# Changes of stage in a hybrid encoder trunk: the second token tile's transposes queued behind the next stage's matmuls with the first

## The chip, the cores and the metric

The kernel runs on one NeuronCore of a Trainium2 chip, with TensorE (matmuls and transposes), VectorE, ScalarE, GpSimd and the DMA queues of that core. The metric is the device time of one execution in microseconds (us); the time before is the median of three runs.

## What is computed

The reference is an encoder of four layers over 256 tokens of 1024 features, in float32. Layer i has a token mixer (0 and 3: a bidirectional Mamba-2 SSD; 1: a bidirectional gated DeltaNet, "gdn"; 2: a bidirectional S5 with a GLU output) and a SwiGLU network ("ffn"). Each is wrapped in two RMS norms:

```python
def rms_norm(x, w):
    y = xf * lax.rsqrt(jnp.mean(xf * xf, axis=-1, keepdims=True) + NORM_EPS)
    return y * w
def reference(x, norm_w, ...):
    h = x
    for i in range(DEPTH):                      # 4
        hn = rms_norm(h, norm_w[i, 0])
        m = mixer(i % 3)(hn)                    # ssd, gdn, s5, ssd
        h = h + rms_norm(m, norm_w[i, 1])
        f = swiglu_ffn(rms_norm(h, norm_w[i, 2]), w_gate_up[i], w_down[i])
        h = h + rms_norm(f, norm_w[i, 3])
    return h
```

## The kernel before

**Data.** The residual `h` stays in SBUF with tokens on partitions, as two token tiles (t = 0 and 1) of 128 tokens. A stage's input is the normed `h`, transposed: features on partitions, 8 chunks k of 128, tokens along the row (256). Products are kept near float32: every operand is split into a high part and the rest, both in float32r, and a product is three matmuls (high by high, high by low, low by high). For activations the parts are `xh` (ScalarE, L191) and `xl` (VectorE, L192), for weights `whi` (ScalarE, L79) and `wlo` (VectorE, L80), from `raw`, which SyncE's queue loads (`weights`, L66 to L82).

**Stages.** ssd0, ffn0, gdn1, ffn1, s5 2, ffn2, ssd3, ffn3, written one after the other. Beside ffn0 and ffn1 run pieces of `s5_prep`, tables for the s5 stage (`s5c`, `tab`, `p`), woven in. A stage ends in `leave` (L226) for each token tile: `rms` (L209: two squares with a sum on ScalarE into a scratch tile, `ms` on VectorE, `rs`, the power -1/2, on GpSimd), then for each half of 512 features `mt` = result times `rs` times norm weight (L236) and `h` = `h` + `mt` (L237). It goes on into the next stage at once. For ffn, `enter_half` (L262) makes `xn` = `h` times norm weight (L266) with the token's scale left for later (`rq`, from `enter_scale`, L269). For the other stages, `enter` (L279) takes a second `rms` first and scales `xn` (L287). `turned` (L249) then transposes `xn`, four blocks into one tile `ht` (L255), and splits it into `xh` and `xl`; for s5 it copies to `s5x`.

**First matmuls of a stage.** In `ffn`, block f takes 8 chunks with 512 weight columns (gate and up of 256 features); tokens are the stationary operand, so one matmul covers one token tile with 512 columns. In block 0 the order is tile 0 for all k (24 matmuls) and then tile 1 (24). In `ssd` and `gdn` `project` (L133) makes the weights the stationary operand and streams all 256 tokens, 128 output features at a time: first the 128 features of dt (`ssd_wdt`, L449) or of a and b (`gdn_wab`, L572), 24 matmuls, then two times 24 for the 256 of `pb` (L466) or `pqk` (L610) of the first group. `dtx` (L451, L574), which the softplus chain on VectorE begins with, reads the first of these.

**Order.** Each engine works through its own queue in a fixed order. The order is set at build time by a scheduler that simulates the program, not by the lines of the source alone; tiles of a pool with few buffers add waits until the buffer's last reader is done.

Of the kernel before, what the change touches and what calls it, by code (L numbers as in the profile page):

```python
# [42 lines left out]
class Trunk:  # L43
    def __init__(self, ctx, tc, t):
        self.tc, self.nc, self.t = tc, tc.nc, t
        nc = self.nc
        pool = lambda name, bufs, **kw: ctx.enter_context(tc.tile_pool(name=name, bufs=bufs, **kw))
        self.cp = pool("const", 1)
        self.wk = pool("wk", 2)
        self.dr = pool("dr", 1, space=bass.MemoryType.DRAM)  # L50
        cp = self.cp
        self.ident = cp.tile([P, P], F32, name="ident")
        nc.gpsimd.dma_start(self.ident, t["c_ident"])
        self.ones = cp.tile([P, 1], F32, name="ones")
# [29 lines left out]
    def mmt(self, out, w, x, first, last, **kw):  # L84

        nc = self.nc
        nc.tensor.matmul(out, x[0], w[0], start=first, stop=False, **kw)  # L87
        nc.tensor.matmul(out, x[1], w[0], start=False, stop=False, **kw)  # L88
        nc.tensor.matmul(out, x[0], w[1], start=False, stop=last, **kw)  # L89

    def mm3(self, out, w, m, x, first, last, **kw):
        nc = self.nc
        hi, lo = (v[:, m * P:(m + 1) * P] for v in w)
        nc.tensor.matmul(out, hi, x[0], start=first, stop=False, **kw)  # L94
        nc.tensor.matmul(out, hi, x[1], start=False, stop=False, **kw)  # L95
        nc.tensor.matmul(out, lo, x[0], start=False, stop=last, **kw)  # L96

# [111 lines left out]
    def rms(self, parts, scale=1.0 / 32):  # L209

        nc = self.nc
        ss = self.wk.tile([P, 2], F32, name="ss", tag="ss", bufs=4)
        for j, p in enumerate(parts):
            sq = self.wide("sq")
            nc.scalar.activation(sq, p, AF.Square, scale=scale, accum_out=ss[:, j:j + 1])
        ms, r = (self.wk.tile([P, 1], F32, name=n, tag=n + "1", bufs=4) for n in ("ms", "rs"))
        nc.vector.scalar_tensor_tensor(out=ms, in0=ss[:, 0:1], scalar=EPS, in1=ss[:, 1:2], op0=ALU.add, op1=ALU.add)  # L217
        nc.gpsimd.tensor_tensor(out=r, in0=ms, in1=self.mhalf[:, 0:1], op=ALU.pow)  # L218
        return r

    def leave_to(self, nxt):


        nc = self.nc

        def leave(t, w, parts, scale=1.0 / 32, q=None):  # L226
            r = self.rms(parts, scale)
            if q is not None:
                r2 = self.wk.tile([P, 1], F32, name="r2", tag="r2", bufs=2)
                nc.vector.tensor_tensor(out=r2, in0=r, in1=q, op=ALU.mult)  # L230
                r = r2
            nw = self.norm_weight(w)
            for j, p in enumerate(parts):
                o = slice(512 * j, 512 * j + 512)
                m = self.wide("mt")
                nc.vector.scalar_tensor_tensor(out=m, in0=p, scalar=r[:, 0:1], in1=nw[:, o], op0=ALU.mult, op1=ALU.mult)  # L236
                nc.vector.tensor_tensor(out=self.h[:, t, o], in0=self.h[:, t, o], in1=m, op=ALU.add)  # L237
                if nxt is None:
                    (nc.sync, nc.scalar)[j].dma_start(self.out[t * P:t * P + P, o], self.h[:, t, o])
                elif nxt[0] == "ffn":  # L240
                    self.enter_half(t, j, nxt[1])
            if nxt is not None and nxt[0] == "ffn":
                self.enter_scale(t)
            elif nxt is not None and nxt[0] != "s5":
                self.enter(t, nxt[1])

        return leave

    def turned(self, t, j, xn, keep=None):  # L249
# [9 lines left out]
        else:  # L259
            self.split(self.xh[:, o[0], o[1]], self.xl[:, o[0], o[1]], pt)  # L260

    def enter_half(self, t, j, w):  # L262

        o = slice(512 * j, 512 * j + 512)
        xn = self.wide("xn")
        self.nc.vector.tensor_tensor(out=xn, in0=self.h[:, t, o], in1=self.norm_weight(w)[:, o], op=ALU.mult)  # L266
        self.turned(t, j, xn)

# [10 lines left out]
    def enter(self, t, w, keep=None):  # L279

        nc = self.nc
        nw = self.norm_weight(w)
        r = self.rms([self.h[:, t, 0:512], self.h[:, t, 512:]])
        for j in range(2):
            o = slice(512 * j, 512 * j + 512)
            xn = self.wide("xn")
            nc.vector.scalar_tensor_tensor(out=xn, in0=self.h[:, t, o], scalar=r[:, 0:1], in1=nw[:, o], op0=ALU.mult,  # L287
                                           op1=ALU.mult)
            self.turned(t, j, xn, keep)


    def ffn(self, i):
        nc, t_ = self.nc, self.t
# [3 lines left out]
        def block(f):  # L297

            w = self.weights(t_["w_gu"][i, f])
            ps = [self.pp.tile([P, 512], F32, name="proj", tag="proj") for _ in range(2)]  # L300
            order = [(t, k) for t in range(2) for k in range(KD)] if f < 1 else [(t, k) for k in range(KD) for t in range(2)]
            for t, k in order:
                self.mmt(ps[t], w[k], (tok(self.xh, k, t), tok(self.xl, k, t)), k == 0, k == KD - 1)
            return ps
# [20 lines left out]
        for f in range(FFB):  # L325
            ps = block(f)
# [106 lines left out]
    def ssd(self, i):  # L433
# [14 lines left out]

        ps = self.project(t["ssd_wdt"][j])  # L449
        x = wk.tile([P, L], F32, name="dtx", tag="t1", bufs=3)  # L450
# [13 lines left out]
        def into(g):  # L464

            pb = self.project(t["ssd_w"][j, g, 2])  # L466
            yield
# [86 lines left out]
    def gdn(self, i):  # L554
# [16 lines left out]

        ps = self.project(t["gdn_wab"])  # L572
        x = wk.tile([P, L], F32, name="dtx", tag="t1", bufs=3)
# [7 lines left out]
        for k in range(2):  # L581
            nc.tensor.transpose(pt[:, k], gb[:, k * P:(k + 1) * P], self.ident)
        gbt = wk.tile([P, 2, P], F32, name="dttok", tag="dttok", bufs=1)
        nc.vector.tensor_copy(gbt, pt)
# [24 lines left out]
        def into(a):  # L609
            pq = self.project(t["gdn_w"][a, 0], name="pqk")  # L610
            yield
# [48 lines left out]
        def base(a):  # L660
# [114 lines left out]
        def apply(a):  # L775
# [159 lines left out]
    def s5_prep(self, pr, first, last):  # L935
# [133 lines left out]
    def s5(self, i):  # L1069
# [179 lines left out]
def trunk(tc, ins, out, steps):  # L1249
    with ExitStack() as ctx:  # L1250
# [8 lines left out]

        k.out, k.rq, k.nwp = out, {}, ctx.enter_context(tc.tile_pool(name="nwp", bufs=2))  # L1260
        pre = lambda kind, i: 4 * i + (2 if kind == "ffn" else 0)
        post = lambda kind, i: pre(kind, i) + 1
        for n, (kind, i) in enumerate(steps):
            np_, nm = BANKS[kind][:2]
            with ExitStack() as c2:
# [106 lines left out]
```

## Time and profile before

| | us |
|---|---|
| median of 3 runs | 2035.88 |
| the runs | 2028.07, 2036.38, 2035.88 |
| the profiled execution | 2029.43 |
| its span, first to last instruction | 2027.7 |
| TensorE busy | 1782.4 |
| VectorE busy | 1441.8 |
| ScalarE busy | 1044.9 |
| GpSimd busy | 353.7 |
| mean granted TensorE clock | 0.932 of full |

The profile is of one execution; all rows shown are from it. A row of a timeline begins with its start in us from the span's start and its duration; consecutive instructions of one kind are one row with a count (x4). Square brackets give how long the engine stood idle before the row and which instruction let it go. A matmul's duration overlaps the next one's, so what one costs in a series is the distance between two starts. PE is TensorE, PEld its weight loads, DVE VectorE, ACT ScalarE, POOL GpSimd, SP SyncE.

### The profile page before, as it was taken

What the parts mean: (1) busy time and instruction counts of PE and PEld (TensorE: products, weight loads), DVE (VectorE), ACT (ScalarE), POOL (GpSimd) and SP (SyncE); (2) the same over time, 40 slices, a digit from 0 to 9 for tenths busy, and PEclk for the clock granted to TensorE, in tenths of its full rate; (3) what the DMA queues carried; (4) which work ended last, traced back from release to release, by engine and by line L of the source; (5) the groups of instructions that cost most, each with busy time, mean ns of one, the idle gap of its engine ahead of it and who ended that gap; (6) DMA issues with size and microseconds to landing.
All of it is one profiled execution on the core that took longest, in us unless ns stands there. A gap on an engine that the chain in (4) does not pass through costs nothing.

```text
span 2027.7 us, 35637 instructions
## 1 busy us (share of the span) xinstructions
PE 1782.4 (88%) x13948; PEld 1526.6 (75%) x13948; DVE 1441.8 (71%) x2542; ACT 1044.9 (52%) x1888; POOL 353.7 (17%) x536
## 2 busy tenths in 40 slices
PE   5999969999599988975999976969997999978998
PEld 5899848888588877763878765658886899857886
DVE  5999957997788676434989458456646999946653
ACT  4777746553466556423545334444434677734442
POOL 1121110000167465621000002010001111110000
PEclk9999979999799999986999966979998999988999
DMA  6344335776344343612767587256644334416652
GB/s 230 118 134 146 115 105 163 243 223 210 120 138 133 99 122 101 182 46 102 236 201 238 175 302 194 68 198 186 187 152 163 125 130 141 127 52 202 185 185 93
DMA packets 105848, 317.66 MB, mean 157 GB/s; under 512 B 11036, under 2 KB 35180, under 8 KB 103632
## 3 DMA queue, kind: packets, MB, share of 16 engines
q1 hardware_dynamic: 99472, 296.03, 45.6%
q0 software_dynamic: 5920, 18.83, 3.1%
q8 instruction: 109, 1.79, 0.4%
q14 instruction: 59, 0.48, 0.1%
q10 hardware_dynamic: 288, 0.52, 0.1%
HBM read 287.49 MB, written 27.85 MB: 156 GB/s over the span
## 4 chain that ended last, share of the span: by engine, by line
PE 71%; DVE 11%; POOL 5%; ACT 5%; issue 4%; DMA 3%; SPq 0%; DVEq 0%; POOLq 0%; ACTq 0%
PE proj L87 10%; PE proj L88 10%; PE proj L89 10%; PE acc_o L87 5%; PE acc_o L88 5%; PE acc_o L89 5%; PE proj L94 5%; PE proj L95 4%; PE proj L96 4%; DVE wlo L80 3%; PE yp L525 2%; POOL ybt L696 2%; ACT whi L79 2%; POOL yb L698 1%; DMA s_w<-wt 1%
## 5 line engine op out<-in xcount | busy, mean ns | idle before, releaser
L80 DVE TENSOR_TENSOR wlo<-raw,whi 128x1024 fp32r<-128x1024 f32 x475 | 599.3, 1267 | 242.2 <-ACT whi L79 235.3
L79 ACT CAST whi<-raw 128x1024 fp32r<-128x1024 f32 x475 | 495.0, 1049 | 413.5 <-PE proj L88 180.8
L87 PE MATMUL proj<-whi,xh 128*128 128x512 f32 x768 | 307.7, 403 | 23.9 <-DVE xl L192 20.0
L89 PE MATMUL proj<-wlo,xh 128*128 128x512 f32 x768 | 304.2, 396 | 0.0
L88 PE MATMUL proj<-whi,xl 128*128 128x512 f32 x768 | 304.2, 396 | 0.0
L94 PE MATMUL proj<-xh,whi 128*128 128x256 f32 x792 | 232.7, 295 | 9.2 <-DVE acc L421 5.0
L96 PE MATMUL proj<-xh,wlo 128*128 128x256 f32 x792 | 229.4, 290 | 0.0
L95 PE MATMUL proj<-xl,whi 128*128 128x256 f32 x792 | 227.3, 287 | 0.0
L87 PEld LDWEIGHTS proj<-whi,xh 128*128 128x128 f32 x768 | 147.2, 192 | 57.5 <-DVE xl L192 21.6
L87 PE MATMUL acc_o<-whi,yh 128*128 128x512 f32 x448 | 179.6, 404 | 5.8 <-ACT yh L191 5.8
L218 POOL TENSOR_TENSOR rs<-ms,mhalf 128x1 f32<-128x1 f32 x32 | 20.9, 653 | 935.0 <-DVE ms L217 930.8
L88 PE MATMUL acc_o<-whi,yl 128*128 128x512 f32 x448 | 179.2, 400 | 0.0
L89 PE MATMUL acc_o<-wlo,yh 128*128 128x512 f32 x448 | 176.3, 396 | 0.0
L89 PEld LDWEIGHTS proj<-wlo,xh 128*128 128x128 f32 x768 | 146.8, 191 | 31.4 <-issue 0.2
L88 PEld LDWEIGHTS proj<-whi,xl 128*128 128x128 f32 x768 | 147.2, 192 | 30.9 <-issue 0.7
L94 PEld LDWEIGHTS proj<-xh,whi 128*128 128x128 f32 x792 | 155.0, 196 | 15.6 <-DVE acc L421 5.8
L95 PEld LDWEIGHTS proj<-xl,whi 128*128 128x128 f32 x792 | 155.3, 196 | 0.1
L96 PEld LDWEIGHTS proj<-xh,wlo 128*128 128x128 f32 x792 | 155.0, 196 | 0.3
L408 ACT ACTIVATE e<-bc,csn 128x256 f32<-128x256 f32 (+1 forms) x320 | 108.7, 430 | 39.0 <-PE bc L403 39.0
L255 PE MATMUL ht<-ident,xn 128*128 128x128 f32 x128 | 29.2, 381 | 108.8 <-DVE xn L287 48.1
L421 DVE SCALAR_TENSOR_TENSOR acc<-proj,cw,acc 128x255 f32<-128x255 f32 (+1 forms) x256 | 118.3, 476 | 2.0
L500 POOL TENSOR_TENSOR e<-e,cbm 128x768 f32<-128x768 f32 x32 | 60.7, 1897 | 324.1 <-DVE cbm L852 130.7
(357 smaller groups left out, 3416.8 us busy)
## 6 DMA issues: line engine op xcount, KB each, us to landing
raw<-w_gu SPq DMA_DIRECT2D x176, 512.0 KB, 4.5
raw<-ssd_w SPq DMA_DIRECT2D x96, 512.0 KB, 3.8
raw<-w_dn SPq DMA_DIRECT2D x88, 512.0 KB, 3.6
raw<-gdn_w SPq DMA_DIRECT2D x48, 512.0 KB, 4.2
raw<-ssd_wo SPq DMA_DIRECT2D x32, 512.0 KB, 3.5
nwb<-norm_w POOLq DMA_DIRECT2D x16, 512.0 KB, 5.1
s_w<-wt SPq DMA_DIRECT2D x16, 512.0 KB, 5.4
s_cl<-clb SPq DMA_DIRECT2D x16, 512.0 KB, 5.2
```

Of the source, the lines that this page charges most:

```text
L79: nc.scalar.copy(hi, raw)
L80: nc.vector.tensor_tensor(out=lo, in0=raw, in1=hi.bitcast(F32), op=ALU.subtract)
L87: nc.tensor.matmul(out, x[0], w[0], start=first, stop=False, **kw)
L88: nc.tensor.matmul(out, x[1], w[0], start=False, stop=False, **kw)
L89: nc.tensor.matmul(out, x[0], w[1], start=False, stop=last, **kw)
L94: nc.tensor.matmul(out, hi, x[0], start=first, stop=False, **kw)
L95: nc.tensor.matmul(out, hi, x[1], start=False, stop=False, **kw)
L96: nc.tensor.matmul(out, lo, x[0], start=False, stop=last, **kw)
L408: nc.scalar.activation(e[:, o], src, AF.Relu, scale=-1.0, bias=n)
L421: nc.vector.scalar_tensor_tensor(out=acc[:, a:b], in0=ps[:, m, a + o:b + o], scalar=cw[:, k:k + 1], in1=acc[:, a:b], op0=ALU.mult, op1=ALU ...
L500: (nc.gpsimd if hl % 2 == 0 else nc.vector).tensor_tensor(out=es[hl], in0=es[hl], in1=cbm, op=ALU.mult)
L525: nc.tensor.matmul(yp[64 * hh:64 * hh + 64, m, a:b], xdt[:, s, d, 2 * m + hh], es[2 * m + hh][:, o:o + b - a], start=(n == 0), stop=(n == 3))
```

## The change

`turn` puts tile 1's transposes on a list; `turn_late` writes them behind the last matmul of the next stage that works on tile 0, with `issue_after`, which orders them on TensorE. In `ffn` that is between the two halves of block 0. For `ssd` and `gdn` the new `project_first` makes the first two projections token tile by token tile: 72 matmuls of 128 columns for tile 0, the transposes, 72 for tile 1. For s5 the transposes stay where they were. `leave` multiplies by the norm weight before `rs` is there, and takes the scale and the addition in one operation. The squares go to one fixed tile, `xn` gets a pool of two buffers, and to make room several tiles share or lose buffers. The weight casts are given no place in the order; the scheduler sets it.

```diff
+        self.junk = cp.tile([P, 512], F32, name="junk")
...
+    def project_first(self, srcs, names):
+
+        ws = [self.weights(v) for v in srcs]
+        out = [self.pp.tile([P, 2, L], F32, name=n, tag="proj") for n in names]
+        for t in range(2):
+            o = slice(t * P, t * P + P)
+            if t:
+                self.turn_late(mm)
+            for w, ps, src in zip(ws, out, srcs):
+                for m in range(src.shape[2] // P):
+                    for k in range(KD):
+                        mm = self.mm3(ps[:, m, o], w[k], m, (self.xh[:, k, o], self.xl[:, k, o]), k == 0, k == KD - 1)
+        return out
...
-            sq = self.wide("sq")
-            nc.scalar.activation(sq, p, AF.Square, scale=scale, accum_out=ss[:, j:j + 1])
+            nc.scalar.activation(self.junk, p, AF.Square, scale=scale, accum_out=ss[:, j:j + 1])
...
             r = self.rms(parts, scale)
+            nw = self.norm_weight(w)
+            ms = [self.wide("mt") for _ in parts]
+            for j, p in enumerate(parts):
+                nc.vector.tensor_tensor(out=ms[j], in0=p, in1=nw[:, 512 * j:512 * j + 512], op=ALU.mult)
...
-            nw = self.norm_weight(w)
-            for j, p in enumerate(parts):
+            for j, m in enumerate(ms):
                 o = slice(512 * j, 512 * j + 512)
-                m = self.wide("mt")
-                nc.vector.scalar_tensor_tensor(out=m, in0=p, scalar=r[:, 0:1], in1=nw[:, o], op0=ALU.mult, op1=ALU.mult)
-                nc.vector.tensor_tensor(out=self.h[:, t, o], in0=self.h[:, t, o], in1=m, op=ALU.add)
+                nc.vector.scalar_tensor_tensor(out=self.h[:, t, o], in0=m, scalar=r[:, 0:1], in1=self.h[:, t, o],
+                                               op0=ALU.mult, op1=ALU.add)
...
+    def turn(self, t, j, xn):
+
+        if t:
+            self.late.append((t, j, xn))
+        else:
+            self.turned(t, j, xn)
+
+    def turn_late(self, last):
+
+        with self.tc.issue_after(last.ins):
+            for v in self.late:
+                self.turned(*v)
+        self.late = []
+
     def enter_half(self, t, j, w):
...
-        xn = self.wide("xn")
+        xn = self.xnp.tile([P, 512], F32, name="xn", tag="xn")
...
-        self.turned(t, j, xn)
+        self.turn(t, j, xn)
...
             for t, k in order:
-                self.mmt(ps[t], w[k], (tok(self.xh, k, t), tok(self.xl, k, t)), k == 0, k == KD - 1)
+                if f < 1 and (t, k) == (1, 0):
+                    self.turn_late(mm)
+                mm = self.mmt(ps[t], w[k], (tok(self.xh, k, t), tok(self.xl, k, t)), k == 0, k == KD - 1)
...
-        ps = self.project(t["ssd_wdt"][j])
+        ps, pb0 = self.project_first([t["ssd_wdt"][j], t["ssd_w"][j, 0, 2]], ("proj", "proj"))
...
-            pb = self.project(t["ssd_w"][j, g, 2])
+            pb = self.project(t["ssd_w"][j, g, 2]) if g else pb0
...
-        ps = self.project(t["gdn_wab"])
+        ps, pq0 = self.project_first([t["gdn_wab"], t["gdn_w"][0, 0]], ("proj", "pqk"))
...
-            pq = self.project(t["gdn_w"][a, 0], name="pqk")
+            pq = self.project(t["gdn_w"][a, 0], name="pqk") if a else pq0
...
-                off = wk.tile([P, 2, P], F32, name="off", tag="off", bufs=7)
+                off = wk.tile([P, 2, P], F32, name="off", tag="off", bufs=6)
...
-            toep = pr.tile([P, P], F32, name="toep", tag="toep", bufs=2)
+            toep = pr.tile([P, P], F32, name="toep", tag="toep", bufs=1)
...
+        k.xnp, k.late = ctx.enter_context(tc.tile_pool(name="xnp", bufs=2)), []
...
-                k.slot = {"gdn": ("u", 3), "s5": ("u1", 2)}.get(kind, ("n5", 4))
+                k.slot = {"gdn": ("u", 3), "s5": ("u1", 2)}.get(kind, ("n5", 2))
```

Left out here: `enter` takes `turn` in the same way unless it keeps `s5x`; `mmt` and `mm3` return their last matmul; `dttok` of gdn shares the buffers of `lx`, `ysq` those of `yo`, and `s5bg` a wide slot. Lines of the changed kernel stand some 15 to 35 further down: `ht` L271, `xh` and `xl` L206 and L207, `whi` and `wlo` L80 and L81, `mt` L245, `h` L252, `xn` L296 and L317, the squares L229.

How the change moves instructions is shown at three places. First, VectorE's queue at the entry into ffn3, from tile 1's residual on (`mt`, `h`: the residual; `xn`: the normed input; `xl`: the low part of the transposed input; `wlo`: low casts of block 0's weights; `g`, `y`: the gate of block 0). Before:

```order
L236 SCALAR_TENSOR_TENSOR mt<-acc_o,rs,nwb 128x512
L237 TENSOR_TENSOR h<-h,mt 128x512
L266 TENSOR_TENSOR xn<-h,nwb 128x512
L236 SCALAR_TENSOR_TENSOR mt<-proj,rs,nwb 128x512
L237 TENSOR_TENSOR h<-h,mt 128x512
L266 TENSOR_TENSOR xn<-h,nwb 128x512
L192 TENSOR_TENSOR xl<-ht,xh 128x4x128
L217 SCALAR_TENSOR_TENSOR ms<-ss 128x1
L80 TENSOR_TENSOR wlo<-raw,whi 128x1024 x5
L192 TENSOR_TENSOR xl<-ht,xh 128x4x128
L80 TENSOR_TENSOR wlo<-raw,whi 128x1024
L312 SCALAR_TENSOR_TENSOR g<-th,proj 128x256
```

and now:

```order
L245 TENSOR_TENSOR mt<-acc_o,nwb 128x512
L231 SCALAR_TENSOR_TENSOR ms<-ss 128x1
L245 TENSOR_TENSOR mt<-proj,nwb 128x512
L252 SCALAR_TENSOR_TENSOR h<-mt,rs,h 128x512 x2
L296 TENSOR_TENSOR xn<-h,nwb 128x512 x2
L81 TENSOR_TENSOR wlo<-raw,whi 128x1024 x5
L231 SCALAR_TENSOR_TENSOR ms<-ss 128x1
L81 TENSOR_TENSOR wlo<-raw,whi 128x1024
L347 SCALAR_TENSOR_TENSOR g<-th,proj 128x256
L348 TENSOR_TENSOR y<-g,proj 128x256
L207 TENSOR_TENSOR xl<-ht,xh 128x4x128 x2
L81 TENSOR_TENSOR wlo<-raw,whi 128x1024 x4
```

The products `mt` stand ahead of `ms`, the low casts are no longer ahead of tile 1's last `xl`, and tile 1's two `xl` now stand behind the gate of tile 0.

Second, ScalarE's queue at the entry into ffn2 (`s5w`: the s5 stage's output of a tile; `sq` and, in the changed kernel, `junk`: the squares; `whi`: high casts of ffn2's weights; `th`: the tanh of the s5 output's gate or of ffn's). Before:

```order
L1229 ACTIVATE th<-proj 128x256
L191 CAST xh<-ht 128x4x128
L215 ACTIVATE sq,ss<-h 128x512 x2
L79 CAST whi<-raw 128x1024
L215 ACTIVATE sq,ss<-s5w 128x512
L191 CAST xh<-ht 128x4x128
L215 ACTIVATE sq,ss<-s5w 128x512
L79 CAST whi<-raw 128x1024 x4
L191 CAST xh<-ht 128x4x128
L215 ACTIVATE sq,ss<-h 128x512 x2
L191 CAST xh<-ht 128x4x128
L79 CAST whi<-raw 128x1024
```

and now:

```order
L1264 ACTIVATE th<-proj 128x256
L206 CAST xh<-ht 128x4x128
L229 ACTIVATE junk,ss<-s5w 128x512
L206 CAST xh<-ht 128x4x128
L80 CAST whi<-raw 128x1024 x2
L229 ACTIVATE junk,ss<-h 128x512
L80 CAST whi<-raw 128x1024
L229 ACTIVATE junk,ss<-h 128x512
L80 CAST whi<-raw 128x1024 x3
L346 ACTIVATE th<-proj,rq 128x256
L206 CAST xh<-ht 128x4x128 x2
L80 CAST whi<-raw 128x1024 x4
```

The second tile's squares of `s5w` have moved ahead of the first high cast, and tile 1's two `xh` behind all six casts and the first tanh of block 0.

Third, TensorE's queue at the start of the program, entry into ssd0. Before:

```order
L255 MATMUL ht<-ident,xn 128x128 x16
L94 MATMUL proj<-xh,whi 128x256 x3
L95 MATMUL proj<-xl,whi 128x256
L96 MATMUL proj<-xh,wlo 128x256
L94 MATMUL proj<-xh,whi 128x256
```

and now, where tile 0's matmuls end:

```order
L95 MATMUL proj<-xh,whi 128x128
L96 MATMUL proj<-xl,whi 128x128
L97 MATMUL proj<-xh,wlo 128x128
L271 MATMUL ht<-ident,xn 128x128 x8
L95 MATMUL proj<-xh,whi 128x128 x2
L95 MATMUL proj<-xh,whi 128x256
L96 MATMUL proj<-xl,whi 128x128
```

The sixteen transposes stood together ahead of the first projection; the second eight now stand behind 72 matmuls of 128 columns.

## Rows read from the trace of the kernel before

**Rows 1.** The page of the profile: busy time by engine, and the chain that ended last.

```profile
PE 1782.4 (88%) x13948; PEld 1526.6 (75%) x13948; DVE 1441.8 (71%) x2542; ACT 1044.9 (52%) x1888; POOL 353.7 (17%) x536
...
PE 71%; DVE 11%; POOL 5%; ACT 5%; issue 4%; DMA 3%; SPq 0%; DVEq 0%; POOLq 0%; ACTq 0%
```

**Rows 2.** Windows table, start and the seven entries; columns: start:end, us, busy (count) by engine, PEclk, DMA share, GB/s.

```profile
26.00:35.50 9.50, 9.50 (x76) 9.50 (x75) 4.85 (x6) 3.42 (x5) 0.00 (x0) 1.00 0.24 79
286.20:304.36 18.16, 3.92 (x17) 2.56 (x17) 16.03 (x26) 10.70 (x21) 5.21 (x9) 0.61 0.56 180
508.80:522.78 13.98, 1.99 (x9) 1.56 (x8) 10.75 (x17) 6.44 (x14) 3.15 (x6) 0.62 0.67 217
937.90:959.20 21.30, 3.81 (x17) 2.46 (x17) 15.02 (x22) 9.72 (x20) 7.79 (x12) 0.60 0.52 170
1163.30:1182.46 19.16, 1.99 (x10) 1.57 (x9) 12.26 (x19) 8.61 (x16) 3.66 (x10) 0.61 0.76 260
1323.90:1343.76 19.86, 3.31 (x17) 2.03 (x15) 14.73 (x23) 12.39 (x23) 7.28 (x11) 0.60 0.72 237
1533.00:1547.55 14.55, 1.94 (x8) 1.57 (x8) 11.58 (x18) 6.95 (x13) 4.06 (x6) 0.61 0.68 238
1811.80:1832.93 21.13, 3.46 (x17) 2.26 (x16) 16.47 (x25) 11.63 (x22) 5.70 (x10) 0.60 0.23 79
```

**Rows 3.** Timeline of TensorE, entry into ffn3; columns: start us, us, engine line op out<-in [idle <-releaser].

```profile
1815.47 0.66 PE L255 MATMUL ht<-ident,xn 128*128 128x128 f32 x4 [1.39 <-DVE xn L266]
1823.26 1.09 PE L255 MATMUL ht<-ident,xn 128*128 128x128 f32 x4 [7.13 <-DVE xn L266]
...
1832.93 0.80 PE L87 MATMUL proj<-whi,xh 128*128 128x512 f32 x1 [6.48 <-DVE xl L192]
...
1834.38 0.63 PE L87 MATMUL proj<-whi,xh 128*128 128x512 f32 x1
1834.81 0.63 PE L88 MATMUL proj<-whi,xl 128*128 128x512 f32 x1
...
1838.17 0.39 PE L87 MATMUL proj<-whi,xh 128*128 128x512 f32 x1
...
1844.97 0.39 PE L87 MATMUL proj<-whi,xh 128*128 128x512 f32 x1
```

**Rows 4.** Timeline of VectorE, the same entry.

```profile
1826.49 5.78 DVE L80 TENSOR_TENSOR wlo<-raw,whi 128x1024 fp32r<-128x1024 f32 x5
1832.20 0.68 DVE L192 TENSOR_TENSOR xl<-ht,xh 128x512 fp32r<-128x512 f32 x1
```

**Rows 5.** Timeline of ScalarE and VectorE, entry into ffn2.

```profile
1327.91 1.04 ACT L79 CAST whi<-raw 128x1024 fp32r<-128x1024 f32 x1 [0.98 <-DMA raw<-w_gu]
...
1331.55 0.16 DVE L230 TENSOR_TENSOR r<-rs,half 128x1 f32<-128x1 f32 x1 [0.69 <-POOL rs L218]
```

**Rows 6.** Timeline of TensorE, a stretch of ssd0 and one of gdn1.

```profile
100.03 0.28 PE L95 MATMUL proj<-xl,whi 128*128 128x256 f32 x1
100.15 0.95 PE L153 MATMUL ss<-ones,ysq 128*128 128x1 f32 x8
100.96 0.36 PE L96 MATMUL proj<-xh,wlo 128*128 128x256 f32 x1
...
887.02 1.16 PE L797 MATMUL pu<-u,off 128*128 128x128 f32 x8
```

**Rows 7.** The page, costliest groups: weight loads of the projections.

```profile
L94 PEld LDWEIGHTS proj<-xh,whi 128*128 128x128 f32 x792 | 155.0, 196 | 15.6 <-DVE acc L421 5.8
```

**Rows 8.** Timeline of VectorE at the entries into gdn1, ffn1 and ssd3.

```profile
511.50 1.28 DVE L192 TENSOR_TENSOR xl<-ht,xh 128x512 fp32r<-128x512 f32 x2
...
962.90 0.76 DVE L940 TENSOR_TENSOR bt<-s5b,tab 128x256 f32<-128x256 f32 x2 [3.75 <-DMA tab<-s_tab]
...
1538.42 0.69 DVE L192 TENSOR_TENSOR xl<-ht,xh 128x512 fp32r<-128x512 f32 x1
```

**Rows 9.** Timeline of VectorE, the last operation before the output's transfers.

```profile
2023.04 1.28 DVE L237 TENSOR_TENSOR h<-h,mt 128x512 f32<-128x512 f32 x2
```

More of the change, by code (lines that the diff above doesn't have):

```diff
@@ L88, in mmt @@
         nc.tensor.matmul(out, x[1], w[0], start=False, stop=False, **kw)
-        nc.tensor.matmul(out, x[0], w[1], start=False, stop=last, **kw)
+        return nc.tensor.matmul(out, x[0], w[1], start=False, stop=last, **kw)
     def mm3(self, out, w, m, x, first, last, **kw):
@@ L95, in mm3 @@
         nc.tensor.matmul(out, hi, x[1], start=False, stop=False, **kw)
-        nc.tensor.matmul(out, lo, x[0], start=False, stop=last, **kw)
+        return nc.tensor.matmul(out, lo, x[0], start=False, stop=last, **kw)
     def halves(self, src, first_y, second_y):
@@ L285, in enter @@
             o = slice(512 * j, 512 * j + 512)
-            xn = self.wide("xn")
+            xn = self.xnp.tile([P, 512], F32, name="xn", tag="xn")
             nc.vector.scalar_tensor_tensor(out=xn, in0=self.h[:, t, o], scalar=r[:, 0:1], in1=nw[:, o], op0=ALU.mult,
                                            op1=ALU.mult)
-            self.turned(t, j, xn, keep)
+            if keep is None:
+                self.turn(t, j, xn)
+            else:
+                self.turned(t, j, xn, keep)
     def ffn(self, i):
@@ L582, in gdn @@
             nc.tensor.transpose(pt[:, k], gb[:, k * P:(k + 1) * P], self.ident)
-        gbt = wk.tile([P, 2, P], F32, name="dttok", tag="dttok", bufs=1)
+        gbt = wk.tile([P, 2, P], F32, name="dttok", tag="lx", bufs=2)
         nc.vector.tensor_copy(gbt, pt)
@@ L813, in apply @@
                         nc.tensor.matmul(po[:, 2 * m + s], es[m][:, x:x + P], uu[v], start=(n == 0), stop=(n == 2))
-            sq = wk.tile([P, 4, P], F32, name="ysq", tag="ysq", bufs=1)
+            sq = wk.tile([P, 4, P], F32, name="ysq", tag="yo", bufs=1)
             nc.scalar.square(sq, po)
@@ L1073, in s5 @@
         nc.gpsimd.dma_start(par, t["s5_d"])
-        bg, sel = wk.tile([4, 512], F32, name="s5bg", tag="s5bg", bufs=1), wk.tile([4, 4, P], F32R, name="s5sel", tag="s5sel", bufs=1)
+        bg, sel = self.wide("s5bg")[0:4], wk.tile([4, 4, P], F32R, name="s5sel", tag="s5sel", bufs=1)
         nc.gpsimd.dma_start(bg, t["s5_bg"])
```

## Prediction

> **What bounds the kernel now.** I read the page first. TensorE is busy for 88% of the span and carries 71% of the chain that ended last; VectorE carries 11%, no other engine more than 5% [rows 1]. So inside the stages the matmuls set the time, and what this change can win lies in stretches where TensorE stands still. The second view, the windows table, was cut at the eight entries into a stage [rows 2]. The first row is the start, where TensorE works without a gap. The other seven run from about the last matmul of one stage to the first of the next (into s5: to tile 1's transposes): 128.2 us together (18.16 + 13.98 + 21.30 + 19.16 + 19.86 + 14.55 + 21.13), in which TensorE does 20.4 us of work (transposes, and a last matmul) at a granted clock of 0.60 to 0.62, while VectorE is busy 64 to 88% of the time. These entries are serial: norm of token tile 0, its transposes, norm of tile 1, its transposes, and only then matmuls.
>
> The third view, TensorE's timeline at the entry into ffn3, shows what the first matmul waits for [rows 3]. Tile 0's transposes are done soon after 1815.47, tile 1's start at 1823.26, and the first matmul at 1832.93 ends an idle stretch of 6.48 us that VectorE's `xl` released. VectorE's own timeline says why that `xl` was late: five low casts of weights, 5.78 us, stand in front of tile 1's second `xl` at 1832.20 [rows 4]. Tile 0 could long have been multiplied.
>
> **Prices.** In ffn the change adds no matmul: block 0 already does tile 0's 24 and then tile 1's 24. A 512-column matmul takes 0.43 us at the lower of the two clock levels, 1.2 and 2.4 GHz (1834.38 to 1834.81), and 0.227 at the higher ((1844.97 - 1838.17)/30) [rows 3]. At the start, in gdn and in ssd3, `project_first` replaces 72 matmuls of 256 columns by 144 of 128, for 216 more in all. A 256-column one takes 0.12 at the higher clock (100.03 to 100.15) [rows 6]; no 128-column one in this number format is in the trace. From below: 0.227 minus 0.12 is 0.107 for 256 columns, so 128 fewer give 0.066. From above: the eight plain float32 matmuls of 128 columns took 1.16 together, 0.145 each [rows 6], and beyond that one weight load, unhidden, has a mean of 0.196 [rows 7]. The nearest row in kind is a matmul of one column with a 128-column weight load: eight from 100.15 to 100.96, 0.10 each [rows 6]. It streams nothing, so 0.10 is what the loads need; I take **0.11**, a little above it, and 0.21 at the lower clock, about twice that.
>
> The Trainium skill ("TensorE: Matmul & The Clock Gate", LDWEIGHTS) has a rule that speaks against this part: a load costs the loaded columns divided by 1.2 GHz, 107 ns for 128, however few columns are then streamed. The one-column row, 0.10, agrees, and by it the sum stays as below.
>
> **The entries, one by one** (gain +, loss -, in us).
> - ssd3 to ffn3: **+5**. On VectorE the residual needs one pass behind `rs` instead of two, and the low casts now come behind tile 1's `xn`, from about 1823.8 instead of 1826.49 [rows 4]. The first cast is out at 1825, so tile 0's 24 matmuls run from 1825 to 1832 (nine at 0.43, fifteen at 0.227, and what they wait for casts). Then 1.2 for transposes, with tile 0's tanh, gate and product ahead of tile 1's `xl` on ScalarE and VectorE: about 1 more. Tile 1 runs 1834.4 to 1839.8 instead of ending near 1845 [rows 3].
> - s5 to ffn2: **+10**. Tile 1's scale `r` came at 1331.55, behind a `whi` cast of 1327.91 that had waited for its weights' transfer [rows 5]. The new order puts tile 1's second square ahead of the casts; `r` moves to 1327.5, tile 1's `xn` ends by 1330.4, casts start there, tile 0 runs 1331.5 to 1338.5 and tile 1 ends near 1345.4. Before, the first matmul came at 1343.76 [rows 2], and block 0 of 48 takes 12.3 from there, as in ffn3 (1832.93 to 1844.97 and 0.23 [rows 3]): 1356.
> - gdn to ffn1: **+3.3**. The same, but tile 1's `xl` now stands behind work for the later s5 stage that waits for `tab` until 962.90 [rows 8]. Its transfer no longer waits for the transposes of tile 1 and should start several us earlier.
> - ssd0 to ffn0: **-1**. First matmul at 304.36 [rows 2] with only 1.4 of waiting; tile 1's `xh` and `xl` now stand behind s5 work that waits for DMAs.
> - ffn1 to s5: **+4.5**. Transposes are as before; the gain is the product ahead of `rs` and no cast between. Bounds: 1.3 (as at the end) and 4.6.
> - ffn0 to gdn: **+1.8**. The first half of tile 0's `xl` is there at 512.1 [rows 8] against 522.78 for the first matmul [rows 2]. Tile 0: 19 matmuls at 0.21, 53 at 0.11, 9.8 us, to 521.8; transposes 1.2; tile 1: 72 at 0.11, 7.9, to 531. Before, 72 full ones ended at 522.78 + 14 x 0.21 + 58 x 0.12 = 532.7 (how many run at the lower clock is an estimate).
> - ffn2 to ssd3: **-0.6**. The same, but tile 0's `xl` comes at 1539.1 [rows 8], only 8.5 ahead of 1547.55 [rows 2].
> - Start: **-7.4**. Tile 1 was hardly behind tile 0; the row from 26.00 has TensorE full for its 9.50 us [rows 2]. Tile 0 can start at about 23.4 and ends 9.8 later, at 33.2; with 1.7 for tile 1's transposes and split, and 7.9 for its 72, the end is 42.8 instead of 35.4, and nothing stands still later to absorb it.
> - End: **+1.3**: the second pass over `h`, 1.28 us, goes [rows 9].
>
> Buffers: the squares' junk tile and the pool for `xn` only loosen waits. `off` with six buffers, `toep` with one and the shared slots I cost at nothing: `off` is written by GpSimd, busy for 17% of the span [rows 1], so a later write has room; `toep` with one buffer waits for its own transfer, on ScalarE, and without slack there its copies would hold casts back by some us.
>
> **Sum**: 5 + 10 + 3.3 - 1 + 4.5 + 1.8 - 0.6 - 7.4 + 1.3 = 16.9. The profiled execution took 2029.43 (span 2027.7), so an execution like it would take 2012.5; it is 6.5 below the median, 2035.88, which would become 2019. The runs shown lie 8 apart, so I name the middle, nearer the median: **2017**. Some 375 of the new matmuls lie on the path at the higher clock, so each 0.01 us of their price is worth 3.75 us, and the gain is gone at 0.11 + 16.9/375 = 0.155.
>
> **Rivals.**
> - *The halved matmuls cost per instruction, and dearly (slower).* Place: the start, gdn, ssd3. If a load doesn't hide behind the matmul before, the price is 0.196 [rows 7], 375 x 0.086 = 32 more than I took, and the time 15 above: 2051. It decides from 0.155. For: the loads' mean is longer than any such matmul's streaming. Against: loads of one-column matmuls follow at 0.10 [rows 6]. Chance 0.17, with all that I don't see.
> - *They cost per column (faster still).* At 0.066 the gain is 16.9 + 375 x 0.044 = 33, the time 2003 by the median and 1996 by the profiled run. Against: the one-column row. Chance 0.15. The Trainium skill, same page, Back-to-back issue gap, gives 81 ns for streams of 128-column matmuls with their loads; by that the gain would be 28. Its figure for 512 columns there, 131 ns, is not what this trace has (0.227).
> - *Tile 1 is late again (no change).* Its `xh` and `xl` now queue behind the gate of tile 0 and, in ffn0 and ffn1, behind DMAs; or, with TensorE stopped between the tiles, its clock drops, and tile 1's 24 matmuls cost 0.2 more each, 4.8 at each of four ffn entries, 19: 2036. Against the clock part: at 1815.47, after 1.39 us of idling, four transposes took 0.66, at 1823.26, after 7.13, 1.09 [rows 3], and the stop I expect is 1 to 2 us. Chance 0.20.
>
> **How the numbers follow.** My case, 0.48, spreads from 2007 to 2028: prices of 0.10 to 0.13 move it by 4 down and 8 up, and the terms on ffn1 and s5 by 3 each. About 10 us, 0.5%, is what a measurement can tell; my case falls short of that in one of eight. Faster: 0.42 + 0.15 + 0.01 of the late tile, 0.58. Same: 0.06 + 0.19, 0.25. Slower: 0.17. The range for 8 in 10 takes the per-column case and the one without change, and leaves out the dear half of the slow one: 1998 to 2042. My case's own range is 2007 to 2028.
>
> **What would show it.** Right: block 0 of ffn3 under way some 7 us earlier, counted from the stage's last matmul, with a second group of eight transposes between 24 and 24; entries into ffn2 and ffn3 shorter by 10 and 5; 128-column matmuls 0.11 apart; the start longer by 7. Wrong: matmuls at 0.13 or more, an idle stretch of over 3 us between the tiles, lower-clock spacing in tile 1's matmuls, or a new idle stretch inside gdn.

## The result: 1% slower, and the profile after

The changed kernel took 2053.99 us (four runs, 2053.39 to 2055.21) against 2033.88 for the kernel before (four runs by now, 2028.07 to 2036.38): a ratio of 1.0104, 95% interval 1.008 to 1.0128, so 20 us slower. I had put 2017 at the head, with a range to 2042.

The page of the changed kernel, busy time by engine and the chain that ended last, answers to [rows 1]:

```profile
PE 1855.7 (90%) x14164; PEld 1598.9 (78%) x14164; DVE 1429.2 (70%) x2542; ACT 1047.2 (51%) x1888; POOL 350.2 (17%) x536
...
PE 71%; DVE 7%; POOL 6%; DMA 5%; issue 5%; ACT 4%; SPq 0%; POOLq 0%; DVEq 0%; ACTq 0%
```

TensorE is busy 73 us longer (1855.7 against 1782.4) in a span only 25.5 us longer: it stands still less, as meant, and works more than was to be added. Cutting both traces at each stage's first transposes shows where:

| stage, from its first transposes to the next stage's, us | before | after | difference |
|---|---|---|---|
| ssd0 | 266.9 | 289.5 | +22.6 |
| ffn0 | 219.8 | 222.1 | +2.3 |
| gdn1 | 431.9 | 449.4 | +17.5 |
| ffn1 | 238.4 | 230.3 | -8.1 |
| s5 | 145.9 | 144.5 | -1.4 |
| ffn2 | 207.6 | 196.7 | -10.9 |
| ssd3 | 282.2 | 293.0 | +10.8 |
| ffn3, to the end of the span | 214.2 | 206.2 | -8.0 |

The three stages that begin with `project_first` lost 51 us; four of the other five won 28. Here is one of the three groups of the projections' matmuls (the low weights), by form (columns: line, engine, operation, out<-in, shape, count, busy us, mean ns of one, idle before):

```profile
L97 PE MATMUL proj<-xh,wlo 128*128 128x128 f32 x112 | 46.5, 415 | 0.0
L97 PE MATMUL proj<-xh,wlo 128*128 128x256 f32 x736 | 212.9, 289 | 0.0
```

A 128-column matmul lasted 415 ns on average, longer than a 256-column one. TensorE's timeline at the start shows what that is in spacing:

```profile
38.42 0.41 PE L95 MATMUL proj<-xh,whi 128*128 128x128 f32 x1
38.63 0.41 PE L96 MATMUL proj<-xl,whi 128*128 128x128 f32 x1
...
56.32 0.41 PE L97 MATMUL proj<-xh,wlo 128*128 128x128 f32 x1
56.53 0.52 PE L96 MATMUL proj<-xl,whi 128*128 128x256 f32 x1
...
60.40 0.28 PE L96 MATMUL proj<-xl,whi 128*128 128x256 f32 x1
60.52 0.28 PE L97 MATMUL proj<-xh,wlo 128*128 128x256 f32 x1
```

The halves are 0.213 us apart, at 38.42 as just ahead of 56.53, after 33 us of matmuls with hardly a gap. Only behind the first full ones, from 56.53 on, does the spacing fall to 0.12, at 60.40; the full ones before that were 0.213 apart too. So it is TensorE's clock. The windows table of the entry into gdn1 says so in its PEclk column (columns as in [rows 2]):

```profile
533.00:539.00 6.00, 1.28 (x9) 0.89 (x9) 5.96 (x9) 4.16 (x8) 1.18 (x2) 0.93 0.48 152
539.00:545.00 6.00, 6.00 (x29) 6.00 (x29) 2.71 (x4) 2.20 (x5) 2.02 (x4) 0.50 0.83 310
545.00:554.00 9.00, 9.00 (x44) 9.00 (x43) 1.50 (x2) 0.20 (x1) 4.08 (x7) 0.50 0.21 73
565.00:571.80 6.80, 6.80 (x34) 6.80 (x34) 6.53 (x11) 1.97 (x4) 0.00 (x0) 0.50 0.23 77
571.80:576.00 4.20, 4.20 (x23) 4.20 (x23) 3.81 (x8) 1.04 (x1) 0.00 (x0) 0.54 0.54 179
576.00:582.00 6.00, 4.96 (x42) 4.63 (x40) 3.11 (x7) 2.66 (x3) 0.00 (x0) 1.00 0.23 76
```

From 539 to 571.8 TensorE works with hardly a pause and the granted clock stays at 0.50, the lower level of 1.2 GHz. It had been at the higher one until the tile's transposes and fell in the 4.6 us that TensorE then waited for `xl`. With full-width matmuls, from 571.8, it is back at 1.00 by 576. At ssd3 the same:

```profile
1562.80:1578.00 15.20, 15.16 (x71) 15.17 (x72) 3.09 (x7) 1.65 (x5) 3.14 (x6) 0.50 0.41 153
1580.00:1595.00 15.00, 15.00 (x71) 14.99 (x71) 5.55 (x7) 3.41 (x5) 0.00 (x0) 0.50 0.11 36
```

(At the start PEclk reads 1.00 in both kernels while the spacing is 0.213: the first change of the clock that the trace records comes at 60.29 us, and before it the column shows the higher level. There the spacing is the better witness.)

The entries without `project_first` went as forecast. TensorE's timeline at the entry into ffn3 answers to [rows 3]:

```profile
1847.05 1.17 PE L271 MATMUL ht<-ident,xn 128*128 128x128 f32 x8 [1.51 <-DVE xn L296]
1854.83 0.77 PE L88 MATMUL proj<-whi,xh 128*128 128x512 f32 x1 [6.62 <-DVE mt L245]
...
1858.58 0.79 PE L90 MATMUL proj<-wlo,xh 128*128 128x512 f32 x1 [2.56 <-DVE wlo L81]
...
1865.54 1.03 PE L271 MATMUL ht<-ident,xn 128*128 128x128 f32 x8
1866.82 0.73 PE L88 MATMUL proj<-whi,xh 128*128 128x512 f32 x2 [0.24 <-ACT xh L206]
...
1872.44 0.39 PE L89 MATMUL proj<-whi,xl 128*128 128x512 f32 x1
```

The first matmul comes 7.8 us behind tile 0's transposes (before: 19.5), waits at 1858.58 for the first low cast, and tile 1's transposes stand behind the 24th. The 48th matmul starts 25.4 us behind tile 0's transposes, against 32.0 before. (Block 0 has 48. Behind late transposes the scheduler puts some of block 1's among them, as the two `whi,xh` at 1866.82 show, so this counts work done and not the end of block 0.)

In ffn0 the late transposes lost. TensorE and then ScalarE there:

```profile
327.16 1.03 PE L271 MATMUL ht<-ident,xn 128*128 128x128 f32 x8
...
334.44 1.22 PE L88 MATMUL proj<-whi,xh 128*128 128x512 f32 x2 [6.24 <-ACT xh L206]
335.46 0.63 PE L89 MATMUL proj<-whi,xl 128*128 128x512 f32 x1
335.89 0.63 PE L90 MATMUL proj<-wlo,xh 128*128 128x512 f32 x1
```

```profile
328.49 0.63 ACT L991 ACTIVATE s5c<-s5c 128x512 f32<-128x512 f32 x1 [6.03 <-DMA s5c<-s_c]
330.60 0.63 ACT L990 ACTIVATE s5c<-s5c 128x512 f32<-128x512 f32 x1 [1.48 <-DMA s5c<-s_c]
...
333.44 0.47 ACT L346 ACTIVATE th<-proj,rq 128x256 f32<-128x256 f32 x1
333.81 1.06 ACT L206 CAST xh<-ht 128x512 fp32r<-128x512 f32 x2
```

Tile 1's transposes at 327.16 are done in a microsecond. Before the next matmul TensorE stands idle for 6.24 us until `xh`, which is queued on ScalarE behind two `s5c` operations that waited 6.03 and 1.48 us for their transfers, two copies of their results and tile 0's tanh. Behind the stop the matmuls are 0.43 us apart, the lower clock's spacing, until 340.15.

### The profile page after: what moved, and what is told of

Same layout as the page of the kernel before. It is cut to its first block, busy times and chain, and to the rows that moved or that the text cites. A ratio compares the mean times of both kernels' runs of the same rounds, so it can differ in the third digit from the quotient of the medians.

```text
span 2053.2 us, 36087 instructions
## 1 busy us (share of the span) xinstructions
PE 1855.7 (90%) x14164; PEld 1598.9 (78%) x14164; DVE 1429.2 (70%) x2542; ACT 1047.2 (51%) x1888; POOL 350.2 (17%) x536
## 4 chain that ended last, share of the span: by engine, by line
PE 71%; DVE 7%; POOL 6%; DMA 5%; issue 5%; ACT 4%; SPq 0%; POOLq 0%; DVEq 0%; ACTq 0%
PE proj L88 9%; PE proj L89 8%; PE proj L90 8%; PE proj L95 6%; PE proj L96 5%; PE proj L97 5%; PE acc_o L88 5%; PE acc_o L89 5%; PE acc_o L90 5%; DVE wlo L81 2%; PE yp L560 2%; POOL yb L733 1%; POOL ybt L731 1%; PE px L1157 1%; DMA yr<-gat 1%
## 5 line engine op out<-in xcount | busy, mean ns | idle before, releaser
L81 DVE TENSOR_TENSOR wlo<-raw,whi 128x1024 fp32r<-128x1024 f32 x475 | 598.2, 1265 | 250.3 <-ACT whi L80 244.7
L80 ACT CAST whi<-raw 128x1024 fp32r<-128x1024 f32 x475 | 495.6, 1050 | 421.1 <-PE proj L89 169.3
L95 PE MATMUL proj<-xh,whi 128*128 128x256 f32 (+1 forms) x848 | 261.3, 310 | 15.2 <-DVE xl L207 12.1
L97 PE MATMUL proj<-xh,wlo 128*128 128x256 f32 (+1 forms) x848 | 259.1, 306 | 0.0
L96 PE MATMUL proj<-xl,whi 128*128 128x256 f32 (+1 forms) x848 | 257.9, 304 | 0.2
L95 PEld LDWEIGHTS proj<-xh,whi 128*128 128x128 f32 x848 | 179.8, 213 | 21.8 <-DVE xl L207 12.6
L96 PEld LDWEIGHTS proj<-xl,whi 128*128 128x128 f32 x848 | 180.6, 213 | 0.7 <-DVE xl L207 0.6
L97 PEld LDWEIGHTS proj<-xh,wlo 128*128 128x128 f32 x848 | 180.6, 213 | 0.3
L89 PEld LDWEIGHTS proj<-whi,xl 128*128 128x128 f32 x768 | 149.0, 194 | 32.2 <-issue 0.9
L456 DVE SCALAR_TENSOR_TENSOR acc<-proj,cw,acc 128x254 f32<-128x254 f32 (+1 forms) x256 | 117.1, 474 | 1.9
L88 PEld LDWEIGHTS acc_o<-whi,yh 128*128 128x128 f32 x448 | 85.6, 192 | 24.1 <-ACT yh L206 6.9
```

What stands on the lines that cost most here:

```text
L80: nc.scalar.copy(hi, raw)
L81: nc.vector.tensor_tensor(out=lo, in0=raw, in1=hi.bitcast(F32), op=ALU.subtract)
L97: return nc.tensor.matmul(out, lo, x[0], start=False, stop=last, **kw)
L456: nc.vector.scalar_tensor_tensor(out=acc[:, a:b], in0=ps[:, m, a + o:b + o], scalar=cw[:, k:k + 1], in1=acc[:, a:b], op0=ALU.mult, op1=ALU ...
```

## The experiments

**1. The first projections whole again.** Edit: the first projections of ssd and gdn by `project` as before, their transposes at once.

```diff
-        ps, pb0 = self.project_first([t["ssd_wdt"][j], t["ssd_w"][j, 0, 2]], ("proj", "proj"))
+        ps = self.project(t["ssd_wdt"][j])
...
-            if keep is None:
-                self.turn(t, j, xn)
-            else:
-                self.turned(t, j, xn, keep)
+            self.turned(t, j, xn, keep)
```

> The changed kernel with the first projections of ssd and gdn whole again (256 columns) and their transposes at once; ffn, the residual and the buffers stay changed. Theory A (the 128-column matmuls are the whole loss: 0.213 us each instead of 0.12 for twice the columns): ssd0, gdn1 and ssd3 come back by 21, 18 and 10 us, the ffn gains stay, 2004 us. Theory B (the loss in ssd and gdn comes from the smaller buffers or the new order on VectorE and ScalarE): at least 2040 us, and the first projections start as late as in the changed kernel.

Measured: 2005.93 us (2005.43 to 2008.38), ratio to before 0.9876 (0.9856 to 0.9896). That is 48 us off the changed kernel and 27 faster than before. Stages as in the table above: ssd0 266.8, gdn1 434.5, ssd3 276.9 (22.7, 14.9 and 16.1 less than in the changed kernel); ffn1, ffn2 and ffn3 within 1 us of the changed kernel. Its windows over the first projections of gdn1 and ssd3:

```profile
533.00:539.00 6.00, 6.00 (x52) 6.00 (x51) 4.38 (x6) 2.97 (x5) 0.00 (x0) 0.99 0.24 87
1542.00:1547.00 5.00, 5.00 (x44) 5.00 (x43) 4.24 (x6) 2.22 (x4) 0.00 (x0) 1.00 0.31 105
```

The clock is up (0.99 and 1.00) where the changed kernel has 0.50. Theory A stands, B falls: with all the change's buffers left in, ssd0 is as fast as before.

**2. ffn's transposes at once, project_first kept.** Edit: `turned` for `turn` in `enter_half`, and no `turn_late` in ffn.

```diff
-                if f < 1 and (t, k) == (1, 0):
-                    self.turn_late(mm)
...
-        self.turn(t, j, xn)
+        self.turned(t, j, xn)
```

> The changed kernel with ffn's transposes of tile 1 at once, as before; project_first, the residual and the buffers stay changed. Theory A1 (the late transposes are what ffn wins): the entries into ffn1, ffn2 and ffn3 lose about 7 us each again, 2074 us. Theory A2 (the residual's new order and the order of casts that came with it win): 2054 to 2060 us.

Measured: 2054.72 us, 1.0112 (1.0089 to 1.0136): the same as the changed kernel, as A2 said. But by stage it isn't nothing: ffn2 201.7 and ffn3 211.3, 5 us longer each; ffn0 2.5 and ffn1 3.5 shorter; and ssd0, 284.3, 5 shorter, gdn1 2.4 shorter, ssd3 3.6 longer. So ffn's four stages lose 4 us in all, and ssd0 gains 5. There TensorE's instructions stand in the same order in both traces, all 1948, and so do those of VectorE, ScalarE and GpSimd. But behind tile 1's transposes the clock rose among the halves:

```profile
40.37 1.01 PE L95 MATMUL proj<-xh,whi 128*128 128x128 f32 x3
41.17 0.35 PE L96 MATMUL proj<-xl,whi 128*128 128x128 f32 x1
41.36 0.27 PE L97 MATMUL proj<-xh,wlo 128*128 128x128 f32 x1
41.47 0.28 PE L95 MATMUL proj<-xh,whi 128*128 128x128 f32 x1
```

Tile 0's halves are 0.213 apart as in the changed kernel; from 41.36, where the trace records the clock as up, tile 1's are 0.111 apart, and the last starts at 48.96 instead of 56.32. With one order of instructions, then, the halves came at either price. In gdn1 and ssd3 all of them stayed at 0.213. The differences in gdn1 and ssd3, whose order changed, I can't give to this edit.

**3. The residual alone.** Both edits together: neither late transposes nor `project_first`; the residual's new order, the scratch tile, `xn`'s pool and the buffers stay.

> Neither late transposes nor project_first; only the residual's new order, the scratch tile, the pool for xn and the buffers are changed. Theory A1 (late transposes win in ffn): close to before, 2022 to 2030 us. Theory A2 (the residual's order wins): 2005 to 2010 us. Theory B (the buffers cost): slower than before, 2040 us or more.

Measured: 2016.0 us (seven runs, 2012.3 to 2026.04), 0.993 (0.9905 to 0.9955): 17 under before, between the two theories. Experiment 1, which differs by the late transposes in ffn, is 10 us faster, but ffn's four stages have only 3.5 of the 7.8 us between the two profiled executions (856.5 against 860.0); gdn1 has 5.3 and ssd3 2.6, which the edit doesn't touch. Entry into ffn3 in this run, and below it in experiment 1 (timelines of TensorE):

```profile
1800.11 1.17 PE L271 MATMUL ht<-ident,xn 128*128 128x128 f32 x8 [1.53 <-DVE xn L296]
1809.97 1.94 PE L271 MATMUL ht<-ident,xn 128*128 128x128 f32 x8 [8.70 <-DVE xn L296]
1817.42 0.79 PE L88 MATMUL proj<-whi,xh 128*128 128x512 f32 x1 [5.52 <-DVE xl L207]
```

```profile
1805.04 0.77 PE L88 MATMUL proj<-whi,xh 128*128 128x512 f32 x1 [6.60 <-DVE mt L245]
...
1815.95 1.04 PE L271 MATMUL ht<-ident,xn 128*128 128x128 f32 x8
1817.22 0.73 PE L88 MATMUL proj<-whi,xh 128*128 128x512 f32 x2 [0.24 <-ACT xh L206]
```

Without them the first matmul comes at +17.3, behind both tiles' transposes; with them at +7.8, and the 48th at +25.6 instead of +30.3. Over the four ffn entries, the start of the 48th matmul, in us from tile 0's transposes ("both" is experiment 1):

| | before | residual alone | both | after |
|---|---|---|---|---|
| ffn0 | 28.7 | 27.2 | 30.4 | 31.5 |
| ffn1 | 32.2 | 24.8 | 27.3 | 26.5 |
| ffn2 | 33.0 | 26.7 | 22.5 | 22.7 |
| ffn3 | 32.0 | 30.3 | 25.6 | 25.4 |

The residual's new order, with the casts it moves, wins in all four (1.5, 7.4, 6.3, 1.7). The late transposes add 4 to 5 in ffn2 and ffn3 and take 3.2 and 2.5 in ffn0 and ffn1, where work for the s5 tables stands ahead of tile 1's split.

**4. Halves in a stretch at the higher clock.** Edit, on the kernel before: one projection in the middle of ssd0 in halves of 128 columns, 96 matmuls for 48.

```diff
-            pb = self.project(t["ssd_w"][j, g, 2])
+            pb = (self.project_halves if g == 4 and i == 0 else self.project)(t["ssd_w"][j, g, 2])
```

> The kernel before, with one projection in the middle of ssd0 (group 4, where the matmuls around it are 0.12 apart) in halves: 96 matmuls of 128 columns for 48 of 256. Theory C1 (such a matmul is load-bound at 0.11 and the clock is only low if it was low before): 0.11 apart, 5 us longer. Theory C2 (such a matmul takes 0.213 at any clock): 0.213 from the first one, and the 256-column ones behind are 0.12 apart at once, 15 us longer. Theory C3 (a stretch of such matmuls lets the clock fall): 0.11 apart at first and 0.213 later, and the first 256-column ones behind it 0.213 apart too, 10 us longer.

The timeline of TensorE near the first of them, at the last, and behind:

```profile
125.56 0.28 PE L95 MATMUL proj<-xl,whi 128*128 128x128 f32 x1
125.67 0.27 PE L96 MATMUL proj<-xh,wlo 128*128 128x128 f32 x1
...
137.75 0.27 PE L95 MATMUL proj<-xl,whi 128*128 128x128 f32 x1
137.86 0.27 PE L96 MATMUL proj<-xh,wlo 128*128 128x128 f32 x1
...
140.56 0.28 PE L94 MATMUL proj<-xh,whi 128*128 128x256 f32 x1
140.68 0.28 PE L95 MATMUL proj<-xl,whi 128*128 128x256 f32 x1
```

0.111 apart from the first to the last, and 0.12 behind: C1's 0.11, and my price. ssd0 took 271.9, 5.0 longer than before. The whole took 2050.56 us, though, 17 more than before, where C1 said 5: gdn1, which the edit doesn't touch, took 10 longer (442.1). Its instructions stand in another order there than before: the scheduler plans the whole program, and a change in one stage gives other orders in later ones. That the order makes those 10 us was not tried by itself.

**5. Late transposes in ffn2 and ffn3 only.** Edit, on experiment 1:

```diff
-        self.turn(t, j, xn)
+        (self.turn if w > 8 else self.turned)(t, j, xn)
```

> As the run with the first projections whole, and late transposes only in ffn2 and ffn3; in ffn0 and ffn1, where pieces of the s5 tables run beside, tile 1's transposes come at once. Theory D1 (there tile 1's split waits behind that work, and late transposes lose 3.2 and 2.5 us by the end of block 0): 2000 us. Theory D2 (they are worth the same in all four): 2010 us or more.

Measured: 2008.86 us (2001.77 to 2010.63), 0.9883 (0.986 to 0.9906), no different from experiment 1. At the entries D1 held: the 48th matmul at +27.2 in ffn0 and +25.7 in ffn1, 3.2 and 1.6 sooner, and ffn's four stages took 852.6 us together against 856.5. (Four us are hardly a sign: before and experiment 4, which leaves ffn alone, differ by as much, 879.9 and 884.2.) The total didn't follow: gdn1 took 443.3 instead of 434.5 and ssd3 282.7 instead of 276.9. On every engine both stand in the order of experiment 3, where they took 439.8 and 279.5, and not in that of experiment 1. Inconclusive for the time.

**6. The clock held up.** Edit: the changed kernel, with matmuls of 512 columns into a bank that nobody reads ahead of `project_first`'s.

```diff
+        warm = self.pp.tile([P, 512], F32, name="warm", tag="proj")
+        for n in range(spare):
+            self.nc.tensor.matmul(warm, ws[0][0][0], self.first_hi, start=n == 0, stop=n == spare - 1)
```

> The changed kernel with extra matmuls of 512 columns, whose result nobody reads, in TensorE's idle time ahead of the first projections of ssd0 (40), gdn1 (22) and ssd3 (32). Theory C1 (the 128-column matmuls cost 0.111 us at the higher clock, keep it there, and the loss is that they start at the lower one and never leave it): they run 0.111 apart in all three places, 15 us less at each, 2008 us. Theory C3 (a long gapless stretch of them lets the clock fall): 0.111 at first, 0.213 within some us, 2030 to 2050 us.

Measured: 2033.6 us (ten runs, 2023.09 to 2049.62), 1.0012 (0.9984 to 1.004): 20 less than the changed kernel, not 46. Windows over the halves at the start (three), at gdn1 and at ssd3:

```profile
24.80:30.00 5.20, 5.20 (x28) 5.20 (x29) 0.41 (x1) 0.00 (x0) 0.12 (x1) 0.55 0.34 104
30.00:39.00 9.00, 9.00 (x44) 9.00 (x43) 0.00 (x0) 0.00 (x0) 0.00 (x0) 0.50 0.00 0
42.40:49.00 6.60, 6.60 (x61) 6.60 (x61) 2.49 (x4) 2.23 (x4) 0.00 (x0) 1.00 0.00 0
536.40:553.70 17.30, 16.78 (x149) 16.36 (x147) 5.36 (x9) 4.03 (x8) 2.92 (x5) 1.00 0.10 32
1550.00:1567.00 17.00, 16.64 (x146) 16.17 (x146) 3.65 (x6) 3.17 (x6) 0.00 (x0) 1.00 0.06 17
```

and TensorE's spacing in ssd3:

```profile
1550.11 0.28 PE L98 MATMUL proj<-xl,whi 128*128 128x128 f32 x1
1550.22 0.27 PE L99 MATMUL proj<-xh,wlo 128*128 128x128 f32 x1
```

In gdn1 and ssd3 all 144 ran at 1.00, 0.111 apart, for 17 us: C1. But the extra matmuls didn't fit the idle time. The scheduler put them behind the arrival of `xl`, where they cost 7.3 us in gdn1 (529.13 to 536.48) and 8.8 in ssd3. And at the start the clock fell at about 25, behind a wait of 1.05 us for `xl`, read 0.50 for the rest of tile 0's halves, and was up again at 42.4, behind tile 1's transposes and while halves were running. The runs scatter by 26 us, against 2 in the changed kernel; why is not shown. So the halves' cost goes with the clock they find, and they may leave it where it is for long. That the clock can't rise among them is not so, here as in experiment 2, and what decides it is open.

**7. Late transposes alone.** Edit: on the kernel before, `turn` and `turn_late` in ffn only (as in the change), with the buffers that they need room from.

> The kernel before with late transposes in ffn alone: the residual and the projections as before, xn in its own pool, three buffers in the shared slot, off, toep and the shared tiles as in the change. Theory A2 (most of ffn's gain comes from the residual's new order): 2025 to 2033 us. Theory A1 (from the late transposes): 2008 to 2018 us.

Measured: 2031.23 us (ten runs, 2020.86 to 2034.75), 0.9982 (0.9964 to 0.9999): next to nothing. With the old residual the 48th matmul came at +29.1, +26.9, +23.8 and +26.6, sooner by 5 to 9 us in the last three than before, but s5 took 154.0 us (145.9 before) and gdn1 440.9 (431.9), and what cost them that is not shown. The total lies where A2 put it, but A2 doesn't follow: ffn's four stages took 858.8 us together, against 879.9 before, 860.0 with the residual alone and 856.5 with both. Either part wins some 20 us in ffn by itself, and the second adds little to the first.

## Why the prediction was wrong

**The step that failed** is in the lines on the start, gdn and ssd3: "19 matmuls at 0.21, 53 at 0.11" for tile 0, and all of tile 1 at 0.11. I let the clock rise behind the first matmuls as it does behind the 256-column ones in the trace of before. Both prices were right: 0.111 at the higher clock in experiments 4 and 6, 0.213 at the lower. What was wrong was how many ran at which: all 432 at the lower one in the profiled execution. By entry (gain +, loss -, us; the three first rows to the last half-width matmul, before to the 72nd full one; ffn to the 48th):

| | forecast | measured |
|---|---|---|
| start | -7.4 | -21.0 (last half at 56.32; before, the 72 end at 35.3) |
| ffn0 to gdn | +1.8 | -13.4 (38.5 behind tile 0's transposes against 25.1) |
| ffn2 to ssd3 | -0.6 | -14.3 (41.7 against 27.4) |
| ssd0 to ffn0 | -1 | -2.8 |
| gdn to ffn1 | +3.3 | +5.7 |
| s5 to ffn2 | +10 | +10.3 |
| ssd3 to ffn3 | +5 | +6.6 |
| ffn1 to s5 | +4.5 | +5.1 (tile 1's transposes 14.4 behind the last matmul against 19.5) |
| end | +1.3 | +1.3 (7.0 behind the last matmul against 8.3) |

At the entry into gdn1 the row of the 72nd matmul before is this one, 25.1 us behind tile 0's transposes at 507.59; in the changed kernel the last half comes at 571.63, 38.5 behind those at 533.10:

```profile
532.74 0.28 PE L96 MATMUL pqk<-xh,wlo 128*128 128x256 f32 x1
```

The six lower rows give 26.2 together where 23.1 was forecast. The three upper give -48.7 where -6.2 was: 42.5 short, and about 1.5 more at each, where full-width matmuls behind the halves run at 0.213 until the clock is up. The sum is -27; the spans differ by 25.5. The number of halves at the lower clock isn't fixed by the kernel, though: by experiment 2 the same start can come out 7 us shorter. (The seven stretches of [rows 2] add to 128.1 us and not 128.2; nothing hangs on it.)

**Steps that held.** The chain at the ffn entries, cast by cast: the first low cast in ffn3 was released 10.3 us behind tile 0's transposes (1857.31 and 1847.05); the forecast had 10.4 (1823.8 against 1813.45). The end:

```profile
2048.51 1.42 DVE L252 SCALAR_TENSOR_TENSOR h<-mt,r,h 128x512 f32<-128x512 f32 x2
```

one pass of 1.42 us behind `r`, where two stood [rows 9]. The buffers cost nothing that shows in ssd0 (266.8 in experiment 1, 266.9 before); for gdn1 and s5 that is not shown.

**The rivals.** The slow rival's time, 2051, was nearly right, and its place, and the threshold: 0.213 is past 0.155. Its mechanism was not, so that nearness is luck: at the higher clock the matmuls cost 0.111 and not the 0.196 of a load that doesn't hide. It was the clock. The late-tile rival had the clock falling, but in ffn, while TensorE stops between the tiles. In ffn2 and ffn3 it doesn't: in ffn3 TensorE goes on at 1866.82 after 0.24 us. In ffn0 and ffn1 it does, behind stops of 6.24 and 3.34 us: some 12 and 8 of the next matmuls are 0.42 to 0.43 apart, where 0.23 is the higher clock's spacing, so about 2.4 and 1.6 us went there. I argued from idle time alone and never asked whether a busy TensorE gets its clock back. The row from 26.00 in [rows 2], all full-width, couldn't answer that, and no other row I had read could: I should have carried the lower price for all 432, 0.213, as an end of the range: 16.9 - 375 x 0.103 = -21.7, 2058 us by the median.

The Trainium skill ("TensorE: Matmul & The Clock Gate", What's actually happening) says that the clock follows activity and not the number of matmuls, so that what comes behind a first stretch runs at the higher level whatever is issued. By that rule the table's three upper rows would have come out near the forecast. The windows at 0.50 over 33 us of halves in gdn1 and ssd3 speak against it, and the start of experiment 2, where the clock rose among halves, doesn't; the measurement decides.

## What to carry to other kernels

Splitting a float32r matmul into halves of 128 columns costs almost twice the time at the higher clock (0.111 against 0.12 for twice the columns), and three and a half times where the clock also stays at the lower level (0.213); so see at which level a split stretch begins, and carry both prices, before counting on what it moves earlier. Reordering that adds no matmul, a product ahead of the norm's scale and ffn's transposes behind the first tile's matmuls, won 27 us here, 1.2%, once it stood alone. Where other work waits for DMAs on the engine that prepares the second tile, keep that tile's split ahead of it: in experiment 5 that brought the 48th matmul 3.2 and 1.6 us forward, though no gain in the whole time is shown.

## What the runs showed that I had not expected

- A busy TensorE at the lower clock: 432 matmuls of 128 columns, three stretches of some 33 us, spacing 0.213, granted clock 0.50 in gdn1 and ssd3; full-width ones behind them were at 0.12 within 4 us. In gdn1 and ssd3 of experiment 6 the same matmuls, begun at the higher level, kept it (1.00 for 17 us). At the start of experiments 2 and 6 the level rose in the midst of them, in experiment 2 with every instruction of the stage in the changed kernel's order.
- At the lower level 128 and 256 columns cost the same, 0.213: only the higher one tells them apart (0.111 and 0.12).
- Every edit reorders later stages too: gdn1 took 432 to 443 us in kernels whose gdn1 has whole projections and differs in nothing but order and buffers. With one order on all engines it took 439.8 and 443.3 (experiments 3 and 5), so some 3 us can go with the execution. Differences under some 10 us between kernels here are read by entry and not by the total.
